# First adaLN chunk and first value weights of the first stage, loaded and multiplied in halves

## The chip, the cores and the metric

The kernel runs on one core of a Trainium2 chip. The core has a matrix engine (PE, or TensorE), a vector engine (DVE), a scalar engine (ACT), a general engine (POOL), and SP, which only issues transfers here. Each engine takes its instructions in a fixed order, and they meet through semaphores. The metric is the device time of one execution in microseconds (us), as the median of several runs.

## The reference

A two-layer backbone over 512 latent tokens and 256 context tokens of width 1024. Each layer first makes, from two conditioning vectors (one for latent, one for context rows), a shift and a scale for every feature, and applies them to the normalised rows:

```python
def adaln_terms(cond, w_ada, b_ada):
    m = jax.nn.silu(cond) @ w_ada + b_ada
    return jnp.split(m, 3, axis=-1)          # shift, scale, gate
...
    xl = rms_norm(h_lat, norm_w[li]) * (1.0 + scale_l[:, None, :]) + shift_l[:, None, :]
    xc = rms_norm(h_ctx, norm_w[li]) * (1.0 + scale_c) + shift_c
...
    au_l, av_l, az_l, bq_l, bk_l, bv_l, bz_l = jnp.split(xl @ w_in, EVEN_SPLITS, axis=-1)
```

The first stage of the kernel computes `xl`, `xc` of layer 0 and, interleaved with it, `av = x @ w_in[:, 512:1024]`, the first of the products with `w_in`. All the rest (gating, differential attention, the second layer, the last norm) comes after that stage and isn't touched.

## The kernel before

Matrices are split into a high part (rounded to the matrix engine's 32-bit format, by ACT) and the low rest (a subtraction, by DVE), so each product takes three matmuls: high·high, high·low, low·high. Names ending in h and l are these two parts: `xh`, `xl` for the features, `wh`, `wl` for weights. Rows are in tiles of 128: six row tiles of tokens (0 to 3 latent, 4 and 5 context), eight tiles of features (`kt`), taken in four pairs j (two tiles i = 0, 1 each).

For each pair j the first stage needs the adaLN chunk j (2 MB of `ada`, in four transfers of 512 KB; before, each of the four holds two tiles of the contraction for all 512 outputs of the chunk: the shift and the scale of both feature tiles) and the value weights of that pair (`wr` from `in_ew`, 512 KB, `wch[j]`). The steps for a pair are: `ada_products` multiplies the chunk with the two conditioning vectors (32 small matmuls, L175, each writing a strip of 32 partitions), DVE copies the rows out (L183), PE turns them (L188), DVE adds and multiplies biases (L198 to L201) into `AD` (shift) and `gT` (scale). Then `turned` turns x (L402), and `modulate_in` makes `xh` on ACT (L414), an unrounded copy `xm` (DVE L418 for latent rows, ACT L420 for context rows) and `xl` on DVE (L423). Last come the value products: `av_first` for the latent rows of pair 0 (L462, 24 matmuls of 128x512), `av_part` otherwise (L79 to L81, through `mm3`).

The order in this place comes from two sources. The block `in_order(ACT, DVE, PE)` fixes the order of these three engines for pair 0 as the code is written; it includes the square sums of the context rows (`ssq_quarter` on ACT, L264; `ssq_vector` on DVE, L381), their root (`rstd_of`, the power on POOL, L156) and their scaling (`normalise`, ACT L395). Behind the block a scheduler of the language orders each engine's instructions by its own estimates. `turn_over(n)` (L446) are n matmuls of the identity whose result nobody reads. `load_w` loads the weights of pair j + 1 into `wr` (two buffers) and `split_w` makes `wh` (ACT L66) and `wl` (DVE L67). SP issues all transfers in program order on one queue: four loads of x, small constants, chunk 0, the value weights of pair 0 (`w0`), the context columns of x, chunk 1, and so on.

Of the kernel before, what the change touches and what calls it, by code (L numbers as in the profile page):

```python
# [11 lines left out]
F32 = mybir.dt.float32  # L12
F32R = mybir.dt.float32r
AF = mybir.ActivationFunctionType
ALU = mybir.AluOpType
# [3 lines left out]
P = 128  # L19
# [11 lines left out]
def tile_backbone(ctx: ExitStack, tc: tile.TileContext, a: dict, out: bass.AP):  # L31
    nc = tc.nc
    PE, ACT, DVE, POOL, SP = nc.tensor, nc.scalar, nc.vector, nc.gpsimd, nc.sync

    cst = ctx.enter_context(tc.tile_pool(name="cst", bufs=1))
    wp = ctx.enter_context(tc.tile_pool(name="wp", bufs=3))
# [72 lines left out]
    ident = cst.tile([P, P], F32, name="ident")  # L109
# [5 lines left out]
    p_bg = pool("bg", "left")  # L115
    p_fill = pool("fill", "right")
    fill(p_fill, "fill2", 136)
    p_in = pool("in", "right")
# [5 lines left out]
    def load_raw(src):  # L124
        raw = wp.tile([P, 1024], F32, tag="raw", name=nm("wr"), bufs=2)
        SP.dma_start(raw, src)
        return raw

    def load_ada(n, pl, bufs):

        res = []
        for c in range(4):
            w = til(pl, [P, 2, 512], F32, "ada", bufs)
            SP.dma_start(w, a["ada"][n, c].rearrange("p (k n) -> p k n", k=2))
            res.append(w)
        return res
# [3 lines left out]
    adab = const("adab", [P, 2, 6, 4])  # L140
    normw = const("normw", [P, 2, 8])
    wch = a["ew"]
    adaw = [load_ada(0, p_in, 12)]
    w0 = load_raw(wch[0])
    for j in range(4):
        load_x(j, 4, 2)
    adaw.append(load_ada(1, p_in, 12))
# [11 lines left out]
    c32 = til(p_bg, [P, 8, 32], F32, "c32")  # L159
# [26 lines left out]
    def ada_rows(li, j, row):  # L186
        ps = tr_ps()
        PE.transpose(ps[:, :P], row, ident)  # L188
        ada_bias(li, j, ps[:, :P].rearrange("p (b v) -> p b v", b=4)[:, :, :2])
# [14 lines left out]

    def ada_chunk(li, j, ws, between=None):
        ada_rows(li, j, ada_products(ws, between))


    ada_rest = [(0, 4), (0, 5), (1, 0)]
# [243 lines left out]
                s = (slice(None), i, slice(t * P, (t + 1) * P))  # L453
                mm3(avb[t], (xh[s], xl[s]), (wh[:, i, :], wl[:, i, :]), j == 0 and i == 0, j == 3 and i == 1)

    def av_first(w, ts):

        (xh, xl), (wh, wl) = XT[0], w
        for n, (x_, w_) in enumerate(((xh, wh), (xh, wl), (xl, wh))):
            for i in range(2):  # L460
                for t in ts:
                    PE.matmul(avb[t], x_[:, i, t * P:(t + 1) * P], w_[:, i, :], start=n + i == 0, stop=False)  # L462


    w0h, w0l = (wp.tile([P, 1024], F32R, tag="w" + s, name=nm("w" + s)) for s in "hl")
# [1 line left out]
    with in_order(ACT, DVE, PE):  # L467
        normalise(0, 0)
        xt0 = []

        def fill_in(kt):
            if kt < 5:
                turn_over(2)
            else:
                i = len(xt0)
                xt0.append(turned(0, 0, i, tr_ps() if i else avb[4]))
        ada_chunk(0, 0, adaw[0], between=fill_in)
        ACT.activation(w0h, w0, AF.Copy)
        turn_over(6)
        modulate_in(0, 0, 0, *XT[0], ps=xt0[0],  # L480
                    between=lambda: DVE.tensor_tensor(w0l, w0, w0h.bitcast(F32), op=ALU.subtract))
        for q in range(1, 4):
            ssq_vector(q, 5)
        second = modulate_in(0, 0, 1, *XT[0], ps=xt0[1], only="h")
        for q in range(4):
            ssq_quarter(xq[q], acc, q, 4, 1 if q else 2)
        rs.append(rstd_of(acc, 4, 2))
        second()
        normalise(1, 0)
        h = normalise(0, 1)  # L490
    ws_in = [(w0h, w0l)]
    w = [x.rearrange("p (k n) -> p k n", k=2) for x in ws_in[0]]
    av_first(w, range(4))
    for i in range(2):
        modulate_in(0, 1, i, *XT[0])
    for j in range(4):
# [44 lines left out]
    for t in range(6):  # L541
        v = gav[t]
# [612 lines left out]
def _layout(i):  # L1155
# [8 lines left out]
    for li in range(2):  # L1164
        W = A["ada_w"][li].T
        for j in range(6):
# [4 lines left out]
            ada.append(W[rows].reshape(4, P, D))  # L1171
            adab.append(A["ada_b"][li][rows])
    r["ada"] = np.stack([w.reshape(512, 4, 2, P).transpose(1, 3, 2, 0).reshape(4, P, 1024) for w in ada])
    r["adr"] = np.concatenate(ada[7:12])
    r["crow"] = np.broadcast_to(c[:, None], (2, P, D))
    r["adab"] = np.stack(adab).reshape(2, 6, 4, P).transpose(3, 0, 1, 2)
# [43 lines left out]
```

## Time and profile before

| | us |
|---|---|
| median of 3 runs (691.6 to 692.15) | 692.09 |
| the profiled execution | 691.32 |
| its span, from the first to the last instruction | 689.4 |
| PE busy in the span | 679.4 (99%) |
| DVE busy | 477.2 (69%) |
| ACT busy | 363.5 (53%) |

The profiled execution has 1.9 us outside its span. The span is one long row of matmuls: PE is busy in 99% of it, and its granted clock is 0.997 of full speed. A busy PE counts a matmul from its start to its modelled end, and matmuls overlap, so the 99% is not a measure of spare time; the waits of PE and the gaps between starts are. The first stage takes about the first 64 us, the rest of the span is not affected by the change in what it computes.

### The profile page before, as it was taken

To read this page: it belongs to the slowest core of one execution; us is meant where nothing else is said; L and a number is where in the kernel's file an instruction comes from. 1 tells how busy PE (TensorE), PEld (TensorE's weight loads), DVE (VectorE), ACT (ScalarE), POOL (GpSimd) and SP (SyncE) were. 2 spreads that over 40 slices of the span, in tenths; PEclk is the share of its full clock that TensorE was granted. 3 is DMA by queue.
4 is the path that set the end of the run, shared out by engine and by line. 5 is a ranking of instruction groups with operands and counts; after the bars stand their busy time and mean duration, and the time that the engine had idled before them with its cause. 6 is when DMAs were issued, how large, how long until landed. Compare 5 with 4: busy or idle time off the path is not lost.

```text
span 689.4 us, 12288 instructions
## 1 busy us (share of the span) xinstructions
PE 679.4 (99%) x5053; PEld 628.9 (91%) x5053; DVE 477.2 (69%) x883; ACT 363.5 (53%) x705; POOL 20.3 (3%) x27
## 2 busy tenths in 40 slices
PE   9999999999999999999999999999999999999996
PEld 8778999989988899898899999988889999999995
DVE  2647839954797947979665328676458898876864
ACT  4956323133567645675534314354458787886422
POOL 1000000010001000010000000010000000000000
PEclk9999999999999999999999999999999999999998
DMA  9965894301101011010623301251210211111402
GB/s 339 408 239 222 307 329 132 114 27 36 62 31 32 0 63 61 32 32 1 244 66 127 99 2 32 63 181 35 88 62 26 68 62 63 31 62 31 123 32 91
DMA packets 20359, 69.90 MB, mean 101 GB/s; under 512 B 3152, under 2 KB 3280, under 8 KB 20304
## 3 DMA queue, kind: packets, MB, share of 16 engines
q1 hardware_dynamic: 20304, 69.13, 28.7%
q8 instruction: 39, 0.64, 0.4%
q14 instruction: 16, 0.13, 0.1%
HBM read 67.02 MB, written 2.10 MB: 100 GB/s over the span
## 4 chain that ended last, share of the span: by engine, by line
PE 91%; DVE 4%; ACT 3%; issue 0%; POOL 0%; POOLq 0%; ACTq 0%; DVEq 0%
PE mm L79 19%; PE mm L81 19%; PE mm L80 19%; PE S L79 5%; PE S L80 5%; PE S L81 5%; PE tr L1024 3%; PE S L663 2%; PE S L665 2%; PE tr L175 2%; PE tr L681 2%; PE S L446 2%; PE S L1002 1%; PE S L1006 1%; PE tr L698 1%; PE tr L293 1%
## 5 line engine op out<-in xcount | busy, mean ns | idle before, releaser
L80 PE MATMUL mm<-xl,wh 128*128 128x512 f32 (+1 forms) x240 | 84.7, 353 | 0.0
L81 PE MATMUL mm<-xh,wl 128*128 128x512 f32 (+1 forms) x240 | 84.5, 352 | 0.0
L79 PE MATMUL mm<-xh,wh 128*128 128x512 f32 (+1 forms) x240 | 84.1, 351 | 0.0
L67 DVE TENSOR_TENSOR wl<-wr,wh 128x1024 fp32r<-128x1024 f32 (+1 forms) x40 | 48.3, 1210 | 38.3 <-ACT wh L66 36.8
L369 ACT ACTIVATE e<-S,s 128x768 f32<-128x768 f32 (+1 forms) x80 | 65.2, 817 | 17.4 <-DVE s L368 17.0
L368 DVE TENSOR_REDUCE s<-S 128x1 f32<-128x768 f32 (+1 forms) x80 | 67.2, 842 | 3.6 <-PE S L1006 1.7
L66 ACT ACTIVATE wh<-wr 128x1024 fp32r<-128x1024 f32 (+1 forms) x40 | 41.8, 1049 | 48.2 <-PE mm L80 21.5
L66 ACT ACTIVATE ah<-tr 128x512 fp32r<-128x512 f32 x76 | 43.9, 595 | 24.9 <-PE tr L681 12.7
L67 DVE TENSOR_TENSOR al<-tr,ah 128x512 fp32r<-128x512 f32 x76 | 50.4, 685 | 7.6 <-ACT ah L66 6.7
L79 PEld LDWEIGHTS mm<-xh,wh 128*128 128x128 f32 x240 | 45.2, 188 | 5.2 <-ACT wh L66 0.2
L79 PE MATMUL mm<-wh,xh 128*128 128x256 f32 (+1 forms) x172 | 49.8, 289 | 0.0
L80 PEld LDWEIGHTS mm<-xl,wh 128*128 128x128 f32 x240 | 45.2, 188 | 4.9
L80 PE MATMUL mm<-wl,xh 128*128 128x256 f32 (+1 forms) x172 | 49.6, 288 | 0.0
L81 PEld LDWEIGHTS mm<-xh,wl 128*128 128x128 f32 x240 | 45.1, 188 | 4.6 <-DVE wl L67 0.2
L81 PE MATMUL mm<-wh,xl 128*128 128x256 f32 (+1 forms) x172 | 49.3, 287 | 0.0
L79 PE MATMUL mm<-wo,xh 128*128 128x256 f32 x144 | 40.6, 282 | 0.0
L81 PE MATMUL mm<-wo,xl 128*128 128x256 f32 x144 | 40.4, 281 | 0.0
L80 PE MATMUL mm<-wo,xh 128*128 128x256 f32 x144 | 40.4, 280 | 0.0
L79 PEld LDWEIGHTS mm<-wh,xh 128*128 128x128 f32 x172 | 32.5, 189 | 0.8 <-issue 0.4
L156 POOL TENSOR_TENSOR s<-s,mhalf 128x6 f32<-128x6 f32 (+4 forms) x15 | 16.0, 1070 | 584.6 <-DVE s L1126 225.2
L81 PEld LDWEIGHTS mm<-wh,xl 128*128 128x128 f32 x172 | 32.4, 189 | 0.5
L80 PEld LDWEIGHTS mm<-wl,xh 128*128 128x128 f32 x172 | 32.4, 188 | 0.5
(337 smaller groups left out, 2008.2 us busy)
## 6 DMA issues: line engine op xcount, KB each, us to landing
ada<-in_ada SPq DMA_DIRECT2D x28, 512.0 KB, 9.1
wr<-in_ew SPq DMA_DIRECT2D x28, 512.0 KB, 3.5
ada<-in_adr SPq DMA_DIRECT2D x12, 512.0 KB, 5.7
wr<-in_ewo SPq DMA_DIRECT2D x8, 512.0 KB, 3.4
wr<-in_owz SPq DMA_DIRECT2D x8, 512.0 KB, 3.6
wr<-in_adr SPq DMA_DIRECT2D x8, 512.0 KB, 3.4
wr<-in_owo SPq DMA_DIRECT2D x8, 512.0 KB, 3.7
xr<-in_x SPq DMA_DIRECT2D x4, 768.0 KB, 7.1
```

The costliest lines, as they stand in the source:

```text
L66: ACT.activation(h, src, AF.Copy)
L67: (eng or DVE).tensor_tensor(l, src, h.bitcast(F32), op=ALU.subtract)
L79: PE.matmul(ps, lh, rh, start=first, stop=False)
L80: PE.matmul(ps, lh, rl, start=False, stop=False)
L81: PE.matmul(ps, ll, rh, start=False, stop=last)
L156: return POOL.tensor_tensor(dst, src, mhalf[:, :n], op=ALU.pow)
L175: PE.matmul(ps[32 * b:32 * b + 32, :P], c32[:, kt, :], ws[kt // 2][:, kt % 2, b * P:(b + 1) * P], start=kt == 0, stop=kt == 7)
L368: mx = DVE.tensor_reduce(nmx[:, :1], v[:, :, :w], axis=AX.XY, op=ALU.max, negate=True)
L369: ACT.activation(e.rearrange("p (c k) -> p c k", k=w), v[:, :, :w], AF.Exp, bias=nmx[:, :1], scale=1.0, accum_out=sm[:, col:col + 1])
L446: PE.matmul(avb[3][:, :P], ident, ident, start=True, stop=True)
L663: PE.matmul(S[:, c, :n], QS[:, m, qs], KS[:, m, k0:k0 + n], start=True, stop=False)
L1024: PE.transpose(ps[:, i * 256 + q * P:i * 256 + (q + 1) * P], es[q][:, (2 * j + i) * P:(2 * j + i + 1) * P], ident)
```

## The change

Chunk 0 is stored in another layout in DRAM: the first two transfers (0 and 1) now hold all eight tiles of the contraction for feature tile i = 0 alone (its shift and its scale), the other two (2 and 3) the same for i = 1. The value weights `w0` are loaded in two transfers of 256 KB, the first half (feature tile 0) between the two halves of the chunk, the second behind them. `half_products(i)` and `half_rows(i)` do for one feature tile what `ada_products` and `ada_rows` did for two, and `av_first(i, ts)` is a generator that yields after each set of four matmuls, so that the products of feature tile 1's shift and scale stand between the value matmuls of feature tile 0. The square sums of the context rows on DVE and ACT move behind the modulation of feature tile 1.

```diff
-    adaw = [load_ada(0, p_in, 12)]
-    w0 = load_raw(wch[0])
+    adaw = [load_ada(0, p_in, 12, (0, 1))]
+    w0 = wp.tile([P, 1024], F32, tag="raw", name=nm("wr"), bufs=2)
+    SP.dma_start(w0[:, :512], wch[0][:, :512])
+    adaw[0] += load_ada(0, p_in, 12, (2, 3))
+    SP.dma_start(w0[:, 512:], wch[0][:, 512:])
...
+    def half_products(i, between=None):
+        ps = tr_ps()
+        for kt in range(8):
+            w = adaw[0][2 * i + kt // 4].rearrange("p k n -> p (k n)").rearrange("p (k n) -> p k n", k=4)
+            for b in range(2):
+                PE.matmul(ps[32 * b:32 * b + 32, :P], c32[:, kt, :], w[:, kt % 4, b * P:(b + 1) * P],
+                          start=kt == 0, stop=kt == 7)
+            if between and kt % 2:
+                between(kt)
+        row = til(p_bg, [P, P], F32, "arow", 2)
+        DVE.tensor_copy(row[:64, :], ps[:64, :P])
+        return row
+
+    def half_rows(i, row):
+        ps = tr_ps()
+        PE.transpose(ps[:, :64], row[:64, :], ident[:64, :64])
+        r = ps[:, :64].rearrange("p (b v) -> p b v", b=2)[:, :, :2]
...
+        DVE.scalar_tensor_tensor(g, r[:, 1, :], adab1[:, 0, 0, i:i + 1], wide(normw[:, 0, i:i + 1]), op0=ALU.add, op1=ALU.mult)
+        DVE.tensor_scalar(AD[:, 0, 0, i, :], r[:, 0, :], adab[:, 0, 0, i:i + 1], None, op0=ALU.add)
...
-    def av_first(w, ts):
-        (xh, xl), (wh, wl) = XT[0], w
-        for n, (x_, w_) in enumerate(((xh, wh), (xh, wl), (xl, wh))):
-            for i in range(2):
-                for t in ts:
-                    PE.matmul(avb[t], x_[:, i, t * P:(t + 1) * P], w_[:, i, :], start=n + i == 0, stop=False)
+    def av_first(i, ts):
+        xh, xl = XT[0]
+        for n, (x_, w_) in enumerate(((xh, w0h), (xh, w0l), (xl, w0h))):
+            for t in ts:
+                PE.matmul(avb[t], x_[:, i, t * P:(t + 1) * P], w_[:, i * 512:(i + 1) * 512], start=n + i == 0, stop=False)
+            yield
...
-        ada_chunk(0, 0, adaw[0], between=fill_in)
-        ACT.activation(w0h, w0, AF.Copy)
+        half_rows(0, half_products(0, between=fill_in))
+        ACT.activation(w0h[:, :512], w0[:, :512], AF.Copy)
         turn_over(6)
-        modulate_in(0, 0, 0, *XT[0], ps=xt0[0],
-                    between=lambda: DVE.tensor_tensor(w0l, w0, w0h.bitcast(F32), op=ALU.subtract))
+        modulate_in(0, 0, 0, *XT[0], ps=xt0[0], between=lambda: DVE.tensor_tensor(
+            w0l[:, :512], w0[:, :512], w0h[:, :512].bitcast(F32), op=ALU.subtract))
+        first = av_first(0, range(4))
+        next(first)
+        row = half_products(1)
+        next(first)
+        half_rows(1, row)
+        next(first)
+        ACT.activation(w0h[:, 512:], w0[:, 512:], AF.Copy)
+        modulate_in(0, 0, 1, *XT[0], ps=xt0[1], between=lambda: DVE.tensor_tensor(
+            w0l[:, 512:], w0[:, 512:], w0h[:, 512:].bitcast(F32), op=ALU.subtract))
+        for _ in av_first(1, range(4)):
+            pass
         for q in range(1, 4):
             ssq_vector(q, 5)
-        second = modulate_in(0, 0, 1, *XT[0], ps=xt0[1], only="h")
         for q in range(4):
             ssq_quarter(xq[q], acc, q, 4, 1 if q else 2)
         rs.append(rstd_of(acc, 4, 2))
-        second()
         normalise(1, 0)
         h = normalise(0, 1)
...
-    av_first(w, range(4))
...
+    r["ada"][0] = ada[0].reshape(2, 2, P, 2, 4, P).transpose(1, 3, 5, 4, 0, 2).reshape(4, P, 1024)
```

In the new file the lines that stay stand lower: `turned` is L431 (before L402), `turn_over` L475 (L446), `xh` L443 (L414), `xm` L447 and L449 (L418, L420), `xl` L452 (L423), the squares on DVE L410 (L381), x scaled on ACT L424 (L395), chunk products L179 (L175); `mm3` keeps L79 to L81. New are L218 (`half_products`), L223 (copy of the rows), L228 (their turning), L234 and L235 (scale and shift), L490 (`av_first`), L507 and L517 (the two halves of `wh` of pair 0), L509 and L518 (of `wl`).

PE, from the end of the first chunk's products to the first value matmuls, before (`ada_115` is the last transfer of chunk 0, `S_186`, `mm_184` and `mm_185` are accumulators of the value products, `x_97` is x of pair 0):

```order
L175 MATMUL tr_234<-ada_115,c_14_139 32x128 x8
L402 MATMUL tr_275<-ident,x_97 128x128 x4
L188 MATMUL tr_282<-ident,arow_280 128x128
L446 MATMUL S_186<-ident 128x128 x6
L462 MATMUL mm_184<-wh_196,xh_38_188 128x512
L462 MATMUL mm_185<-wh_196,xh_38_188 128x512
L462 MATMUL S_186<-wh_196,xh_38_188 128x512 x2
L462 MATMUL mm_184<-wh_196,xh_38_188 128x512
L462 MATMUL mm_185<-wh_196,xh_38_188 128x512
```

The same place on PE now (`ada_109` and `ada_111` hold feature tile 0, `ada_115` and `ada_117` feature tile 1):

```order
L218 MATMUL tr_235<-ada_111,c_14_140 32x128 x4
L431 MATMUL tr_260<-ident,x_97 128x128 x4
L228 MATMUL tr_267<-ident,arow_265 128x64
L475 MATMUL S_187<-ident 128x128 x6
L490 MATMUL mm_185<-wh_197,xh_38_189 128x512
L490 MATMUL mm_186<-wh_197,xh_38_189 128x512
L490 MATMUL S_187<-wh_197,xh_38_189 128x512 x2
L218 MATMUL tr_287<-ada_115,c_14_140 32x128 x8
L218 MATMUL tr_287<-ada_117,c_14_140 32x128 x8
L490 MATMUL mm_185<-wl_198,xh_38_189 128x512
L490 MATMUL mm_186<-wl_198,xh_38_189 128x512
L490 MATMUL S_187<-wl_198,xh_38_189 128x512 x2
```

Half of the chunk's products, and one of two turnings of 64 columns, have moved behind the first four value matmuls.

DVE, from `xm` of feature tile 0 to the context rows' square sums, before (`jk` are the squares, the two rows with `s_317` sum and scale them for the root on POOL):

```order
L418 TENSOR_SCALAR xm_294<-S_187,gT,AD 128x512
L481 TENSOR_TENSOR wl_197<-wr_117,wh_196 128x1024
L423 TENSOR_TENSOR xl_39_189<-xm_294,xh_38_188 128x512
L381 SCALAR_TENSOR_TENSOR jk_299,s_145<-x_98 128x256
L381 SCALAR_TENSOR_TENSOR jk_301,s_145<-x_99 128x256
L381 SCALAR_TENSOR_TENSOR jk_303,s_145<-x_100 128x256
L268 TENSOR_REDUCE s_317<-s_145 128x2
L270 TENSOR_SCALAR s_317<-s_317 128x2
L418 TENSOR_SCALAR xm_305<-tr_275,gT,AD 128x512
L423 TENSOR_TENSOR xl_39_189<-xm_305,xh_38_188 128x512
```

The same place on DVE now:

```order
L452 TENSOR_TENSOR xl_39_190<-xm_278,xh_38_189 128x512
L223 COPY arow_304<-tr_287 64x128
L234 SCALAR_TENSOR_TENSOR gT<-tr_310,adab_145,normw_sb 128x2
L235 TENSOR_SCALAR AD<-tr_310,adab_sb 128x2
L447 TENSOR_SCALAR xm_319<-tr_260,gT,AD 128x512
L518 TENSOR_TENSOR wl_198<-wr_113,wh_197 128x512
L452 TENSOR_TENSOR xl_39_190<-xm_319,xh_38_189 128x512
L410 SCALAR_TENSOR_TENSOR jk_336,s_146<-x_98 128x256
L410 SCALAR_TENSOR_TENSOR jk_338,s_146<-x_99 128x256
L410 SCALAR_TENSOR_TENSOR jk_340,s_146<-x_100 128x256
L297 TENSOR_REDUCE s_352<-s_146 128x2
L299 TENSOR_SCALAR s_352<-s_352 128x2
```

The square sums of the context rows stand behind `xm`, `wl` and `xl` of feature tile 1, where they stood ahead of its `xm` and `xl`.

ACT, behind the block that fixes the order, before (`wr_370` are the value weights of pair 1, `wr_498` those of pair 2; `xh_40` is `xh` of pair 1; `x_99` and `x_100` are x of pairs 2 and 3):

```order
L66 ACTIVATE wh_372<-wr_370 128x1024
L395 ACTIVATE x_99<-x_99,s_180 128x256 x4
L395 ACTIVATE x_99<-x_99,s_319 128x256 x2
L414 ACTIVATE xh_40_190<-tr_424,AD,gT 128x512
L414 ACTIVATE xh_40_190<-tr_433,AD,gT 128x512
L395 ACTIVATE x_100<-x_100,s_180 128x256 x2
L414 ACTIVATE xh_40_190<-tr_442,AD,gT 128x256
L395 ACTIVATE x_100<-x_100,s_180 128x256
L414 ACTIVATE xh_40_190<-tr_449,AD,gT 128x256
L420 ACTIVATE xm_445<-tr_442,AD,gT 128x256
L420 ACTIVATE xm_452<-tr_449,AD,gT 128x256
L66 ACTIVATE wh_500<-wr_498 128x1024
```

The same place on ACT now (`wr_379` is pair 1, `wr_507` pair 2):

```order
L66 ACTIVATE wh_381<-wr_379 128x1024
L424 ACTIVATE x_99<-x_99,s_181 128x256 x4
L424 ACTIVATE x_99<-x_99,s_354 128x256 x2
L66 ACTIVATE wh_509<-wr_507 128x1024
L443 ACTIVATE xh_40_191<-tr_433,AD,gT 128x512
L443 ACTIVATE xh_40_191<-tr_442,AD,gT 128x512
L424 ACTIVATE x_100<-x_100,s_181 128x256 x3
L443 ACTIVATE xh_40_191<-tr_451,AD,gT 128x256
```

The scheduler has put the high part of pair 2's weights ahead of `xh` of pair 1; on DVE the low part (`wl_510`, L67) stands in the same way ahead of `xm` of pair 1. From the last value matmuls of the stage on, the engines' orders are the same as before.

## Rows read from the trace of the kernel before

**Rows 1.** The page, block 1: busy us, share of the span, instructions.
```profile
PE 679.4 (99%) x5053; PEld 628.9 (91%) x5053; DVE 477.2 (69%) x883; ACT 363.5 (53%) x705; POOL 20.3 (3%) x27
```

**Rows 2.** Waits of PE, whole span: line, releaser, us in total, times, longest.
```profile
PE tr L402 <- ACT x L395: 0.4, 1, 0.4
PE tr L188 <- DVE arow L183: 0.2, 1, 0.2
```

**Rows 3.** Windows: stretch, length, busy by engine, granted clock, DMA share, GB/s.
```profile
17.50:25.00 7.50, 7.11 (x33) 4.96 (x37) 5.57 (x14) 6.84 (x21) 0.70 (x1) 1.00 1.03 410
...
683.00:685.00 2.00, 0.00 (x0) 0.00 (x0) 1.14 (x4) 0.51 (x2) 0.48 (x1) 1.00 0.00 0
...
686.00:687.50 1.50, 0.00 (x0) 0.00 (x0) 0.00 (x0) 0.00 (x0) 0.00 (x0) 0.50 0.62 257
```

**Rows 4.** Chain that ended last, in time: start, us, engine, tile, line.
```profile
11.21 0.57 PE tr L175 x16
11.79 0.64 PE S L446 x4
...
14.22 0.59 PE S L402 x4
...
20.05 1.05 DVE jk L381 x6
...
30.16 0.23 PE S L81
```

**Rows 5.** Timeline, 15 to 18 us: start, us, engine, line, operation, idle before and releaser.
```profile
15.20 1.06 ACT L478 ACTIVATE wh<-wr 128x1024 fp32r<-128x1024 f32 x1 [2.25 <-DMA wr<-in_ew]
...
15.80 0.32 PE L188 MATMUL tr<-ident,arow 128*128 128x128 f32 x1
...
15.96 1.50 PE L446 MATMUL S<-ident 128*128 128x128 f32 x12
16.16 0.16 DVE L198 TENSOR_TENSOR AD<-tr,adab_sb 128x4 f32<-128x4 f32 x1 [0.42 <-PE tr L188]
...
16.43 0.16 DVE L201 TENSOR_TENSOR gT<-gT,normw_sb 128x4 f32<-128x4 f32 x1
16.69 0.78 ACT L414 ACTIVATE xh<-S,AD,gT 128x512 fp32r<-128x512 f32 x1 [0.43 <-DVE gT L201]
...
17.52 0.73 PE L462 MATMUL mm<-wh,xh 128*128 128x512 f32 x2
```

**Rows 6.** Timeline, 17.5 to 27 us.
```profile
17.50 0.81 DVE L418 TENSOR_SCALAR xm<-S,gT,AD 128x512 f32<-128x512 f32 x1 [0.91 <-ACT xh L414]
...
18.23 1.22 DVE L481 TENSOR_TENSOR wl<-wr,wh 128x1024 fp32r<-128x1024 f32 x1
...
19.36 0.69 DVE L423 TENSOR_TENSOR xl<-xm,xh 128x512 fp32r<-128x512 f32 x1
19.50 0.30 PEld L462 LDWEIGHTS mm<-wl,xh 128*128 128x128 f32 x2 [0.28 <-DVE wl L481]
...
21.63 0.70 POOL L156 TENSOR_TENSOR s<-s,mhalf 128x2 f32<-128x2 f32 x1 [10.41 <-DVE s L270]
...
22.37 1.31 ACT L395 ACTIVATE x<-x,s 128x256 f32<-128x256 f32 x3 [0.64 <-POOL s L156]
...
23.70 0.56 ACT L414 ACTIVATE xh<-tr,AD,gT 128x256 fp32r<-128x256 f32 x1
...
24.87 1.95 PE L175 MATMUL tr<-ada,c 128*32 128x128 f32 x64
```

**Rows 7.** Timeline, 25 to 35 us: pair 1, and the weights of pairs 1 and 2.
```profile
25.91 1.06 ACT L66 ACTIVATE wh<-wr 128x1024 fp32r<-128x1024 f32 x1
...
29.44 1.45 ACT L414 ACTIVATE xh<-tr,AD,gT 128x512 fp32r<-128x512 f32 x2
...
33.88 1.06 ACT L66 ACTIVATE wh<-wr 128x1024 fp32r<-128x1024 f32 x1
```

**Rows 8.** Transfers issued from 21.8 to 22.0 us: times, KB each, us to landing.
```profile
wr<-in_ew SPq DMA_DIRECT2D x1, 512.0 KB, 10.2
```

More of the change, by code (lines that the diff above doesn't have):

```diff
@@ L127, in load_raw, with load_ada @@
         return raw
-    def load_ada(n, pl, bufs):
+    def load_ada(n, pl, bufs, parts=range(4)):
         res = []
-        for c in range(4):
+        for c in parts:
             w = til(pl, [P, 2, 512], F32, "ada", bufs)
@@ L206, in ada_chunk, with wide @@
         ada_rows(li, j, ada_products(ws, between))
+    def half_products(i, between=None):
[14 more added lines that the diff above has]
+        r = ps[:, :64].rearrange("p (b v) -> p b v", b=2)[:, :, :2]
+        def wide(x):
+            return x.to_broadcast([P, 2])
+        g = gT[:, 0, i, :]
+        DVE.scalar_tensor_tensor(g, r[:, 1, :], adab1[:, 0, 0, i:i + 1], wide(normw[:, 0, i:i + 1]), op0=ALU.add, op1=ALU.mult)
+        DVE.tensor_scalar(AD[:, 0, 0, i, :], r[:, 0, :], adab[:, 0, 0, i:i + 1], None, op0=ALU.add)
     ada_rest = [(0, 4), (0, 5), (1, 0)]
@@ L491, in tile_backbone @@
     ws_in = [(w0h, w0l)]
-    w = [x.rearrange("p (k n) -> p k n", k=2) for x in ws_in[0]]
-    av_first(w, range(4))
     for i in range(2):
```

## The prediction

> **What bounds the kernel now.** I read the page's busy times first: PE 679.4 of 689.4 us, every other engine far below [rows 1]. So what a change gives or costs is what it does to the row of PE's matmuls: work added to it, work taken from it, and gaps. Then PE's waits: over the whole span only single short ones are named, and two of them, 0.4 and 0.2 us, lie in the first stage [rows 2]. Then the stage itself, in the chain and the timeline [rows 4 to 7]. Transfers run at 410 GB/s there with all engines of the queue busy, and the clock is granted in full [rows 3]. Behind the stage PE waits for almost nothing, and the order there is unchanged, so a shift of PE at the end of the first stage, about 64 us, is a shift of the end of the kernel. The sum is made there.
>
> **Start of the value products (a gain of 0.95 us).** Before, PE goes at 11.21 through four groups of chunk products (0.57 each), two of two identity matmuls (0.64) and two of four turnings (0.59): 11.21 + 2.28 + 1.28 + 1.18 = 15.95 [rows 4]. Now each group has half its matmuls. A group of 16 records isn't half as long when halved: the 64 records of the next chunk take 1.95 us with a tail of some 0.27, so 0.026 each [rows 6], 0.42 for 16, and the rest of the 0.57 is the switch. Half a group is then 0.21 + 0.15, say 0.37 (bounds 0.285 and 0.57). Four of them save 0.8 (0 to 1.14): the turning of the rows stands at 15.15. Three small DVE steps from 16.16 to 16.59, the last waiting for the one ahead [rows 5], become two that don't wait for each other: 0.18 less. So `xh`, 16.69 before, starts at 15.71, takes 0.78, and the first value matmul comes at 16.55 instead of 17.52 [rows 5]. The six identity matmuls ahead, 1.50 long with the tail, move with the turning and end at 16.5: they only just don't bind. The transfers allow it: all of `w0` landed at 15.2 [rows 5], and at 410 GB/s its first half lands two chunk transfers (1.28 each) and half a weight transfer (0.64) earlier, near 12.0, three us ahead of its use.
>
> **Work that moves behind that start (+1.2).** Sixteen chunk products (32 records, 0.83) now stand after the first four value matmuls, with a switch into and out of them (0.18 each). The bounds are 0.83 and two whole groups plus a switch, 1.3. The chunk's last transfer lands half a weight transfer ahead of 15.2, at 14.6, long before 17.7, when it is needed.
>
> **The chain of feature tile 1 (+0.6).** From 16.55: four matmuls at 0.23 [rows 4] to 17.5, products to 18.5, four with `wl` from 18.7 to 19.65, then the turning of the second rows. Its scale is ready on DVE 0.6 later (0.36 from the turning to the first step, as from 15.80 to 16.16 [rows 5], and 0.25 for two), at 20.25; `xh` of tile 1 takes 0.78, to 21.05. PE has four matmuls in the meantime, to 20.65: it waits 0.4. Four with high weights end at 22.0. Those with the low weights need `xm` (0.73 to the next start, 17.50 to 18.23 [rows 6]) and half of a subtraction of 1.22, at most as long as the 0.69 of `xl` [rows 6]: 21.1 + 0.73 + 0.69 = 22.5, a wait of 0.5. Before, one wait of 0.28 stood in this stretch [rows 6]. 0.4 + 0.5 - 0.3 = 0.6 (0 to 1.2).
>
> **The context rows (+1.8).** This is the largest term, and the change makes it by the place of the square sums. `xl` of tile 1 ends on DVE at 23.1. Only then come three squares (1.05 for them, [rows 4]), the sum and its scaling (0.45, 21.1 to POOL's start at 21.63 with their gaps), the power on POOL (0.70) [rows 6], and the first context tile on ACT (0.5): 23.1 + 1.05 + 0.45 + 0.7 + 0.05 + 0.5 = 25.9. PE has finished all 24 value matmuls by 24.4, and the next in its row is the turning of those tiles: a wait of 1.5, against 0.4 now [rows 2]. Before, four value matmuls (0.93) stood behind these turnings and covered the 0.56 of the context `xh` [rows 6]. Now that cover is gone, since the value matmuls have all been done, and PE waits for it, 0.7 with the hand-over. 1.5 + 0.7 - 0.4 = 1.8 (0.9 if ACT and DVE overlap better than I add them, 2.2 if worse).
>
> **Pair 1 (a gain of 0.2).** The wait of 0.2 for the copied rows [rows 2] goes, since PE comes later to it (0 to 0.2).
>
> **Pair 2's weights ahead of pair 1 (+1.4).** In the new order ACT makes the high part of pair 2's weights before `xh` of pair 1. Before, from POOL's end at 22.33 to the start of pair 1's weights on ACT is 3.6 us, and from there to `xh` of pair 1 3.5 [rows 6, 7]. From 25.35 now, ACT would be free for `xh` at 32.4. Pair 2's weights, issued at 21.89, land 10.2 later, at 32.1 [rows 8]; so ACT hardly waits for them, but spends 0.95 of the 1.06 [rows 7] on them, and `xh` ends at 34.05. PE reaches the matmul that needs it at 33.25 by the same count (27.3, when it goes on after the context rows, and 12 matmuls, the 64 records and nine turnings, with a wait of 0.14): a wait of 0.8. On DVE the low part (1.22) stands ahead of `xm` of pair 1, which frees the two banks for the next turnings: two more waits, 0.45 and 0.15. Together 1.4 (0 if PE is later than I count; one for one more if the transfer lands later). Nothing else is new on SP: pair 2's load waits for DVE's second half, until 22.5 instead of 21.89, and eight transfers are queued ahead of it.
>
> **Sum.** -0.95 + 1.2 + 0.6 + 1.8 - 0.2 + 1.4 = +3.85. On the profiled execution's 691.32 that is 695.2; it ran 0.77 under the median, so on the median of 692.09 it is **695.9**.
>
> One page speaks against the split of the load. In this trace transfers queue: a load issued at 21.89 needs 10.2 us to land because others are ahead of it [rows 8], and the stretch moves 410 GB/s [rows 3], so one more transfer of the same bytes costs nothing here. The Trainium skill, "DMA: Bandwidth & Descriptors", section "Anatomy of one DMA", gives each transfer of the software path a fixed cost of about 2.0 us. By that, if it held for this queue and didn't overlap, pair 2's weights would land 2 us later; the trace does not bear it out, but a late landing is a rival below, priced from rows.
>
> **Rivals.** (a) Pair 2's conversion is covered, because PE gets to pair 1 later than I count: the sum loses 1.4, +2.45, 694.5. For it: my count of PE there is the longest in the working; against it: the same count would have to be 0.8 too short. (b) Pair 2's weights land later. The landing at 32.1 is right at ACT's need at 32.35, so every further us is a us for PE; with the length of a 512 KB transfer and a half (1.9), +1.6 more: 697.5. Against it: the bytes and their order ahead of it are the same. (c) **Faster**: the early start stands and the vector chain closes behind it. It decides at the context turnings: if the power on POOL is done by the time PE has its 24 matmuls behind it, 24.4 less 0.5, so by 23.9 instead of 25.35, and tile 1's chain by 0.5 earlier, PE keeps 0.95, pays 0.35 for the switches alone (the products themselves only moved), and loses the waits of before (0.3 + 0.4 + 0.2): 692.09 - 0.95 + 0.35 - 0.9 = 690.6. Against it: the chain is a sum of measured durations on one engine after the other, and 1.45 us of 3 would have to vanish. (d) Halfway between, near no change. (e) The clock falls in the new gaps. At the end of the span PE does nothing from 683 on; the clock is still granted in full to 685, and is 0.50, its level of 1.2 GHz, from 686 to 687.5 [rows 3]. My longest gap is 1.5 us, between full rows of work. If it fell, a matmul of 0.23 would take twice that; over some thirteen of them +3, so 698.9. The Trainium skill, "TensorE: Matmul & The Clock Gate", section "Why this matters for your kernels", asks for no longer idle gaps between bursts of matmuls; by that rule these gaps are too short, and the sum stays.
>
> **How the numbers follow.** Forecast 0.62, (a) 0.15, (b) 0.09, (c) 0.07, (d) 0.04, (e) 0.03. The forecast's own range, with its bounds, is 694.6 to 697.2. The range has to take in (a) with its lower bounds and (b): 693.2 to 697.8, which leaves out (c), (d), (e) and the tails. A measurement of this kernel tells 0.2%, 1.4 us, from no change. Slower by more than that: forecast, (a), (b), (e) less their low ends, 0.86; the same 0.07; faster 0.07.
>
> **What the changed profile would show.** First value matmul (L490) at 16.5 to 16.7. Its second set of four behind the products at 18.7. PE's waits: for ACT x (L424) about 1.5 at the context turnings near 26, 0.7 behind it, 0.4 and 0.5 in tile 1. ACT's conversion of pair 2's weights (L66) at 32.3, with `xh` of pair 1 right behind it near 33.3, and L79 of pair 1 near 34.0 after a wait of 0.8. The first 128x256 matmul 3.5 to 4 us later than before, and from there on the same distances as before. The sum would be wrong if that lag shrank later, that is if something behind the stage had been waiting for a fixed time, or if the waits for the context rows are not there.

## The result, and the profile after

The changed kernel takes 698.88 us (median of four runs, 698.21 to 699.62) beside 692.12 of the kernel before: 1.0104 times as long, interval 1.0092 to 1.0116. That is slower, as forecast, but by 6.8 us and not by 3.85, and outside the range of 693.2 to 697.8. The profiled execution took 698.21, its span 696.0 (691.32 and 689.4 before).

The timeline of the changed kernel (start us, us, engine, line, operation, in brackets the idle time ahead and what ended it); its rows answer [rows 4 to 7]:

```profile
10.31 0.63 PE L218 MATMUL tr<-ada,c 128*32 128x128 f32 x8
10.87 0.71 PE L475 MATMUL S<-ident 128*128 128x128 f32 x4
...
15.83 0.78 ACT L443 ACTIVATE xh<-S,AD,gT 128x512 fp32r<-128x512 f32 x1 [2.27 <-DVE AD L235]
...
16.66 0.73 PE L490 MATMUL mm<-wh,xh 128*128 128x512 f32 x2
...
17.78 1.94 PE L218 MATMUL tr<-ada,c 128*32 128x128 f32 x32
...
22.36 0.73 PE L490 MATMUL mm<-wh,xh 128*128 128x512 f32 x2 [0.17 <-ACT xh L443]
...
23.80 0.73 PE L490 MATMUL mm<-wl,xh 128*128 128x512 f32 x2 [0.25 <-DVE wl L518]
...
25.93 0.70 POOL L160 TENSOR_TENSOR s<-s,mhalf 128x2 f32<-128x2 f32 x1 [14.63 <-DVE s L299]
...
27.23 0.84 PE L431 MATMUL tr<-ident,x 128*128 128x128 f32 x4 [1.30 <-ACT x L424]
...
28.62 0.79 PE L79 MATMUL S<-wh,xh 128*128 128x512 f32 x1 [0.55 <-ACT xh L443]
...
29.77 2.94 PE L179 MATMUL tr<-ada,c 128*32 128x128 f32 x64
...
33.56 1.05 ACT L66 ACTIVATE wh<-wr 128x1024 fp32r<-128x1024 f32 x1
...
35.20 1.45 ACT L443 ACTIVATE xh<-tr,AD,gT 128x512 fp32r<-128x512 f32 x2 [0.59 <-DVE gT L205]
...
38.66 0.50 PE L79 MATMUL S<-wh,xh 128*128 128x512 f32 x1 [0.44 <-ACT xh L443]
...
69.92 0.28 PE L79 MATMUL mm<-wh,xh 128*128 128x256 f32 x1
```

Four things are to be seen. A group of half the products (8 records, two for each of its four matmuls) stands 0.56 ahead of what follows it, where a whole group of 16 took 0.57 [rows 4]; the second half's 32 records take 1.94, as long as the 64 of a whole chunk [rows 6]. PE waits for the context rows, 1.30 and 0.55. Right behind that, the same 64 records take 2.94 instead of 1.95. And the first 128x256 matmul, with which the rest of the kernel begins, comes at 69.92 instead of 63.95: 5.97 of the 6.6 by which the span grew lie in the first stage.

The windows of the changed kernel (length, busy time of the engines, then the granted clock, DMA share, GB/s) say why the 64 records took longer (the first row is for later):

```profile
4.50:6.00 1.50, 1.50 (x15) 1.50 (x15) 0.78 (x4) 0.91 (x4) 0.00 (x0) 1.00 1.01 407
...
26.00:27.00 1.00, 0.00 (x0) 0.00 (x0) 0.00 (x0) 0.33 (x1) 0.64 (x1) 1.00 1.02 406
27.00:28.00 1.00, 0.77 (x4) 0.40 (x4) 0.00 (x0) 0.98 (x3) 0.00 (x0) 1.00 1.03 401
28.00:29.00 1.00, 0.45 (x2) 0.38 (x2) 0.00 (x0) 1.00 (x3) 0.00 (x0) 0.71 1.03 414
29.00:31.00 2.00, 2.00 (x26) 1.27 (x29) 0.85 (x2) 2.00 (x5) 0.00 (x0) 0.50 1.02 408
31.00:32.00 1.00, 1.00 (x32) 0.94 (x28) 0.70 (x1) 1.00 (x4) 0.00 (x0) 0.58 1.04 414
32.00:40.00 8.00, 7.56 (x63) 5.89 (x52) 5.04 (x11) 7.20 (x16) 0.00 (x0) 1.00 1.02 406
```

PE's busy time (first number behind the length) is 0.00, 0.77 and 0.45 in the three us from 26 on; in the third of them the clock falls (0.71 on average), and behind them it is 0.50, its level of 1.2 GHz. Summed over the windows the clock is missing 0.29 + 2 x 0.50 + 0.42 = 1.7 us.

### The profile page after: what moved, and what is told of

Same layout as the page of the kernel before. It is cut to its first block, busy times and chain, and to the rows that moved or that the text cites. A ratio compares the mean times of both kernels' runs of the same rounds, so it can differ in the third digit from the quotient of the medians.

```text
span 696.0 us, 12298 instructions
## 1 busy us (share of the span) xinstructions
PE 683.5 (98%) x5054; PEld 631.2 (91%) x5054; DVE 477.5 (69%) x886; ACT 363.9 (52%) x706; POOL 20.3 (3%) x27
## 4 chain that ended last, share of the span: by engine, by line
PE 92%; DVE 4%; ACT 3%; issue 0%; POOL 0%; POOLq 0%; ACTq 0%; DVEq 0%
PE mm L79 19%; PE mm L81 19%; PE mm L80 19%; PE S L79 5%; PE S L81 5%; PE S L80 5%; PE tr L1060 3%; PE S L699 2%; PE S L701 2%; PE tr L179 2%; PE S L475 2%; PE tr L717 1%; PE S L1038 1%; PE S L1042 1%; PE tr L734 1%; PE tr L322 1%
## 5 line engine op out<-in xcount | busy, mean ns | idle before, releaser
L81 PE MATMUL mm<-xh,wl 128*128 128x512 f32 (+1 forms) x240 | 84.4, 352 | 0.0
L79 PE MATMUL mm<-xh,wh 128*128 128x512 f32 (+1 forms) x240 | 84.3, 351 | 0.0
L67 DVE TENSOR_TENSOR wl<-wr,wh 128x1024 fp32r<-128x1024 f32 (+1 forms) x40 | 48.2, 1208 | 37.6 <-ACT wh L66 36.0
L67 DVE TENSOR_TENSOR al<-tr,ah 128x512 fp32r<-128x512 f32 x76 | 50.3, 684 | 7.7 <-ACT ah L66 6.7
L79 PE MATMUL mm<-wh,xh 128*128 128x256 f32 (+1 forms) x172 | 49.8, 290 | 0.0
L79 PEld LDWEIGHTS mm<-xh,wh 128*128 128x128 f32 x240 | 45.2, 188 | 5.1 <-ACT wh L66 0.2
L81 PEld LDWEIGHTS mm<-xh,wl 128*128 128x128 f32 x240 | 45.2, 188 | 4.8
L81 PE MATMUL mm<-wh,xl 128*128 128x256 f32 (+1 forms) x172 | 49.3, 288 | 0.0
L79 PE MATMUL mm<-wo,xh 128*128 128x256 f32 x144 | 40.6, 282 | 0.0
L81 PE MATMUL mm<-wo,xl 128*128 128x256 f32 x144 | 40.4, 281 | 0.0
L79 PEld LDWEIGHTS mm<-wh,xh 128*128 128x128 f32 x172 | 32.5, 189 | 0.9 <-ACT vnh L66 0.2
L81 PEld LDWEIGHTS mm<-wh,xl 128*128 128x128 f32 x172 | 32.4, 189 | 0.5
```

Of the source, the lines that this page charges most:

```text
L67: (eng or DVE).tensor_tensor(l, src, h.bitcast(F32), op=ALU.subtract)
L79: PE.matmul(ps, lh, rh, start=first, stop=False)
L81: PE.matmul(ps, ll, rh, start=False, stop=last)
```

## The experiments

Differences are each to the kernel before on the same chip (691.2 to 692.1).

| | us | to before | ratio, interval |
|---|---|---|---|
| changed kernel | 698.88 | +6.8 | 1.0104 [1.0092, 1.0116] |
| e1 squares early | 694.41 | +2.6 | 1.0041 [1.0027, 1.0054] |
| e2 gap filled, ten | 698.48 | +6.7 | 1.0106 [1.0092, 1.0119] |
| e3 four strips | 694.93 | +3.1 | 1.0051 [1.0038, 1.0063] |
| e4 before, groups in two passes | 691.63 | -0.2 | 1.0000 [0.9991, 1.0009] |
| e5 before, late squares | 693.86 | +2.7 | 1.0038 [1.0025, 1.0050] |
| e6 chunk whole, weights in halves | 692.72 | +1.5 | 1.0019 [1.0011, 1.0028] |
| e7 e1 and e3 together | 693.94 | +2.7 | 1.0044 [1.0032, 1.0056] |
| e8 early start | 692.03 | +0.8 | 1.0014 [1.0005, 1.0023] |
| e9 pair 2's weights held | 697.60 | +5.6 | 1.0082 [1.0069, 1.0095] |
| e10 gap filled, five | 696.24 | +4.2 | 1.0062 [1.0049, 1.0074] |
| e11 early start 2 | 690.29 | -1.8 | 0.9975 [0.9966, 0.9983] |
| e12 before, long rows in two passes | 700.41 | +8.4 | 1.0119 [1.0105, 1.0134] |

### What half the products cost

The theory: the four strips of 32 partitions that a chunk's products write work side by side, and time goes by the matmuls of one strip. The rival, on which the prediction had counted: each record costs its 0.026.

**e3, four strips.**

```diff
+                r0 = 32 * (b + 2 * (kt % 2))
-                PE.matmul(ps[32 * b:32 * b + 32, :P], ..., start=kt == 0, stop=kt == 7)
+                PE.matmul(ps[r0:r0 + 32, :P], ..., start=kt < 2, stop=kt > 5)
...
-        PE.transpose(ps[:, :64], row[:64, :], ident[:64, :64])
+        PE.matmul(ps[:, :64], row, ident2, start=True, stop=True)
```

> The changed kernel with its half products spread over four strips of 32 partitions instead of two: even contraction tiles write strips 0 and 1, odd ones strips 2 and 3, and the turning of the rows becomes a matmul with two stacked identities of 64, which also adds the two sums. The number of product matmuls is the same, with half as many one behind the other in each strip. Theory A (strips run side by side, a group costs by its contraction steps in one strip): the first half's four groups of 0.57 become some 0.33 each, and the second half's 16 products take 1.0 instead of 1.94; -0.9 and -0.9 as far as PE is the bound there, 698.9 - 1.8 = 697.1, less if the vector chain takes it over. Rival B (a product costs by itself, wherever it is written): the groups stay at 0.57 and 1.94, 698.9.

Its timeline:

```profile
11.80 0.42 PE L221 MATMUL tr<-ada,c 128*32 128x128 f32 x8
12.15 0.71 PE L478 MATMUL S<-ident 128*128 128x128 f32 x4
...
18.51 1.08 PE L221 MATMUL tr<-ada,c 128*32 128x128 f32 x32
...
27.08 0.84 PE L434 MATMUL tr<-ident,x 128*128 128x128 f32 x4 [1.30 <-ACT x L427]
...
28.46 0.50 PE L79 MATMUL S<-wh,xh 128*128 128x512 f32 x1 [0.55 <-ACT xh L446]
...
29.12 1.96 PE L181 MATMUL tr<-ada,c 128*32 128x128 f32 x64
```

The same 8 records now take 0.35 to the next start instead of 0.56, the same 32 take 1.08 instead of 1.94. Theory A. The kernel gained 3.7 and not 1.8; the waits for the context rows are the same 1.30 and 0.55, but the 64 records behind them take 1.96: the clock stayed full in this profile. That, 1.7, and a wait of 0.44 in pair 1 that is gone (under e9) are about the rest.

**e4, the groups of before in two passes.**

```diff
+    def two_passes(ws, between):
...
+        for c in range(4):
+            for h in range(2):
+                for k in range(2):
+                    for b in range(2 * h, 2 * h + 2):
...
-        ada_chunk(0, 0, adaw[0], between=fill_in)
+        ada_rows(0, 0, two_passes(adaw[0], fill_in))
```

> The kernel before, with each of the four groups of chunk 0's products (two contraction tiles by four strips) in another order: strips 0 and 1 for both contraction tiles, then strips 2 and 3 for both. The same matmuls, none added. Theory A (time goes by contraction steps, the strips side by side, so two strips cost as much as four): a group of 0.57 takes about 1.05, four of them +1.9 on the path to the first value matmul: 692.1 + 1.9 = 694.0. Rival B (0.026 for each of a group's records and a fixed switch, as the prediction counted): the groups stay at 0.57, 692.1. Rival C (the groups get longer but transfers or the vector chain behind them hide it): longer groups, and 692.1 to 693.

```profile
11.25 0.66 PE L193 MATMUL tr<-ada,c 128*32 128x128 f32 x16
11.84 0.71 PE L460 MATMUL S<-ident 128*128 128x128 f32 x4
```

0.59 for a group, 691.63: no change, as rival B had it, and a miss for what I had concluded from theory A. It doesn't bring back B's price for a record, which e3 excludes. A group has two matmuls in each strip in either order. So the matmuls for two strips that stand ahead do not, in a group of eight, keep the other two strips idle.

**e12, the long rows of before in two passes.**

```diff
+            todo = [(kt, b) for h in (0, 2) for kt in range(8) for b in (h, h + 1)]
-        for kt in range(8):
-            for b in range(4):
+        for kt, b in todo:
```

> The kernel before, with the products of every chunk that is multiplied in one uninterrupted row of 32 matmuls (64 records) in another order: strips 0 and 1 for all eight contraction tiles, then strips 2 and 3. The same matmuls. Six chunks of the whole kernel. Theory A (strips run side by side only as far as the next matmul in the row can start; sixteen matmuls of two strips ahead block the others): a row takes 3.7 instead of 1.95, and the kernel 691.2 + 6 x 1.8 = 702. Rival B (each strip has its own row and the order is of no account): 1.95 each, 691.2.

The groups by line (busy us, mean ns) of the kernel before and of this one, all chunk products in each, and one of its rows in the timeline:

```profile
L175 PE MATMUL tr<-ada,c 128*32 128x128 f32 x448 | 14.3, 275 | 0.0
```

```profile
L178 PE MATMUL tr<-ada,c 128*32 128x128 f32 x448 | 22.3, 275 | 0.0
```

```profile
24.25 3.29 PE L178 MATMUL tr<-ada,c 128*32 128x128 f32 x64
```

3.29 instead of 1.95 a row, 8.0 more for all (22.3 against 14.3), 8.4 more measured. With sixteen matmuls in two strips ahead, the others do idle, though less than fully (3.9 would be twice). Two half passes one behind the other would take 2 x 0.63 = 1.26 for a group and 2 x 1.94 = 3.88 for a row; measured are 0.66 (e4) and 3.29. Each time has a short tail, which the sums count twice, so some 0.5 to 0.6 is saved in both. A limit on how far ahead in its row PE starts matmuls of idle strips would give that; no run shows the limit itself. The Trainium skill, "TensorEngine Tiling (Array Packing)", section "Key Properties", says that tiles operate independently and that different ones can run matmuls in parallel; the 1.08 against 1.94 agrees, the 3.29 doesn't, and for a row in that order the measurement decides.

**e6, chunk whole, weights in halves.** `load_ada(0, p_in, 12)`, `ada_chunk` and the old layout again; `av_first`, the loads of `w0` and the late squares stay.

> The changed kernel with the chunk whole again (its layout, one row of 32 products, one turning of the rows); the weights stay in halves, the value matmuls in two sets, the squares late. Theory A (the half products are the largest cost: 1.94 for the second half, with nothing saved on the first): PE loses 1.94 of products and one turning, the chain of tile 1 loses its wait for rows, so the context rows come some 2.5 earlier and the clock stays full: 698.9 - 1.9 - 0.4 - 1.7 = 694.9, the remaining difference from before being the late squares. Rival B (the split of the weights is what costs, the products only move): 697 to 698.9.

692.72, 2.2 less than theory A's number. Its first value matmul is at 17.64, its context turnings wait 0.42 and 0.55 behind them, and the clock is full. So the halves of the chunk carry 5.3 of the 6.8, with all that follows from them (the order of pair 2's weights, under e9, too); halving weights and value matmuls costs 1.5 with the late squares included.

### The wait for the context rows, and the clock

**e5, late squares in the kernel before.** `second()` is called ahead of the squares.

> The kernel before with one part of the change alone: the square sums of the context rows stand behind feature tile 1's modulation. Nothing is halved. Theory A (the place of the squares is a cost by itself): three squares of 0.35 on DVE start 1.4 later, the power on POOL too, and the context turnings come about 24.3 instead of 22.9; the last value matmuls fill some 0.4 of it, so a wait of 0.8 to 1.3 and 0.5 for xh behind it: 691.8 + 1.0 to 1.6 = 693.1. Rival B (the squares cost only in company with the late second half; here the value matmuls still queued cover it): 691.8 to 692.2, no wait above 0.5.

Its timeline and windows:

```profile
24.36 0.84 PE L402 MATMUL tr<-ident,x 128*128 128x128 f32 x4 [0.88 <-ACT x L395]
25.75 0.50 PE L79 MATMUL S<-wh,xh 128*128 128x512 f32 x1 [0.55 <-ACT xh L414]
...
26.41 3.37 PE L175 MATMUL tr<-ada,c 128*32 128x128 f32 x64
```

```profile
27.00:30.00 3.00, 3.00 (x54) 2.62 (x46) 1.83 (x3) 3.00 (x8) 0.00 (x0) 0.50 1.01 404
...
252.00:255.00 3.00, 3.00 (x16) 3.00 (x16) 0.19 (x2) 0.60 (x1) 1.32 (x1) 0.51 0.00 0
```

Theory A: waits of 0.88 and 0.55, as counted. The runs also give the clock's price within one kernel. Those with a mean clock of 0.997 and 0.998 took 692.76 and 692.65; three with 0.995 took 693.7 to 694.2; the profiled one, 0.992 with the two falls above, took 695.69. So some 1.3 to 1.5 each, if those with 0.995 had one fall, and a fall in some executions of a kernel, not in all.

**e1, squares early in the changed kernel.** `ssq_vector` and `ssq_quarter` move ahead of `av_first(0, ...)`, `rstd_of` behind `half_rows(1, row)`.

> The changed kernel with one part undone: the square sums of the context rows on DVE and ACT go back ahead of feature tile 1's modulation (behind feature tile 0's), their root stands behind the second half's rows; halves of the chunk and of the weights stay. Theory A (the late squares make the gap of 1.3 us ahead of the context turnings and 0.55 behind them, and the clock falls because of these): both gaps shrink to under 0.5 together, the clock stays granted in full to 32 us, so 1.4 for the gaps and 1.7 for the 3.41 us at half clock go: 698.9 - 3.1 = 695.8. Rival B (the clock falls for another reason, the halves themselves): only the gaps go, 697.5, and a stretch of 3.4 us at 0.50 is still there. Rival C (three squares of 0.35 on DVE ahead of the second half's rows only push the waits into tile 1's chain): 698.9, with new waits of PE at the value matmuls near 22 to 24.

```profile
27.35 0.60 PE L431 MATMUL tr<-ident,x 128*128 128x128 f32 x4
28.53 0.50 PE L79 MATMUL S<-wh,xh 128*128 128x512 f32 x1 [0.58 <-ACT xh L443]
...
29.20 1.95 PE L179 MATMUL tr<-ada,c 128*32 128x128 f32 x64
```

The wait of 1.30 is gone, the second of 0.58 stays, the clock is full: 4.2 less, to +2.6. Theory A, and 1.4 below its number; pair 2's weights, which stand elsewhere in this run (under e9), can be a part of that.

**e2 and e10, the gap filled.**

```diff
         for _ in av_first(1, range(4)):
             pass
+        for _ in range(10):                  # e10: range(5)
+            PE.matmul(avb[4][:, :P], ident, ident, start=True, stop=True)
```

> The changed kernel and nothing undone; ten more identity matmuls, whose result nobody reads, stand on PE between the last value matmul and the context turnings, where PE has a gap of 1.3 us. They do no useful work. Theory A (the gap lets the clock fall): the granted clock stays at 1.00 from 26 to 32 us, the context turnings start within 0.2 of where they did, and the 3.41 us at half clock are given back: 698.9 - 1.7 = 697.2. Rival B (the clock falls for what stands ahead of it or behind it, not for this gap): the same stretch at 0.50, 698.9 or a little more.

In e2 the clock was granted in full there, but ten such matmuls took 2.23 us (26.39 to 28.62), longer than the gap of 1.3 that they were to fill. Behind them stands a wait of 1.22, since the scheduler set the conversion of pair 1's weights (28.89, 1.04 us on ACT) ahead of the context `xh` here. What the clock gave was lost to these two: 698.48, inconclusive by its time.

> The changed kernel with five identity matmuls (ten were too many: they took 2.25 us and pushed the context turnings 0.85 past their time) in the gap of 1.3 ahead of the context turnings. They do no useful work. Theory A (the clock's fall costs 1.7 for each 3.41 us, and the filled gap prevents it): no stretch at 0.50 between 20 and 40 us, and 698.9 - 1.7 = 697.2. Rival B (the clock's share is smaller than that; the ten matmuls lost nothing beyond it): 698.5 again.

The timeline of e10:

```profile
11.04 0.63 PE L218 MATMUL tr<-ada,c 128*32 128x128 f32 x8
...
17.39 0.73 PE L490 MATMUL mm<-wh,xh 128*128 128x512 f32 x2
...
26.53 1.28 PE L523 MATMUL S<-ident 128*128 128x128 f32 x10
27.99 0.95 PE L431 MATMUL tr<-ident,x 128*128 128x128 f32 x4 [0.18 <-ACT x L424]
29.64 0.50 PE L79 MATMUL S<-wh,xh 128*128 128x512 f32 x1 [0.70 <-ACT xh L443]
...
30.30 1.96 PE L179 MATMUL tr<-ada,c 128*32 128x128 f32 x64
...
34.35 1.45 ACT L443 ACTIVATE xh<-tr,AD,gT 128x512 fp32r<-128x512 f32 x2
35.69 1.05 ACT L66 ACTIVATE wh<-wr 128x1024 fp32r<-128x1024 f32 x1
```

The context turnings come no earlier behind the first value matmul than in the changed kernel (10.60 against 10.57), all the work is there and more, and the kernel is 2.6 faster. Not all of that is the clock: the wait of 0.44 in pair 1 isn't there, because the scheduler set pair 2's weights (35.69) behind the first two `xh` of pair 1, as e9 below does by hand. That leaves some 2. Against e9 itself, which has that order and whose clock fell, e10 is 1.4 faster, with an interval of some 1.2 to either side. So the fall that the gap had cost is worth 1.4 to 2. Theory A. All six runs had a mean clock of 0.998 or 0.999; the four of the changed kernel 0.994 to 0.996.

### Pair 2's weights

**e9, held back** with `issue_after` behind the first two `xh` of pair 1.

> The changed kernel with pair 2's weight conversion held back behind the first two xh of pair 1, on ACT and with it on DVE; nothing else. Theory A (as the trace of the changed kernel reads: ACT waited for gT, so the conversion was covered on ACT, and only DVE's low part stands ahead of xm of pair 1, with one wait of 0.44): 698.9 - 0.4 = 698.5. Rival B (as the prediction counted): -1.4, 697.5. Rival C (nothing at all): 698.9.

The wait of 0.44 for `xh` in pair 1 is gone; from the first matmul behind chunk 1's products to the first 128x256 matmul the profile has 36.80 us instead of 37.29, so 0.5. The clock fell here too, from 30 to 33. The median is 1.3 lower, its interval some 1.2 wide to either side, so time alone doesn't tell A from B; the rows tell for A. Nor does the clock alone set a run's time: one run with a mean clock of 0.999 took 697.13, one with 0.994 took 697.01.

The scheduler chooses this order anew for each version. In e1, e3, e6, e7 and e10 pair 2's weights stand behind the first two `xh` of pair 1 without having been held, and the wait of 0.44 is gone. So what those runs gained over the changed kernel has e9's 0.5 in it (1.3 by the medians), beside what their edits did.

### Both causes undone, and a version that uses the halves

**e7, e1's and e3's edits together.**

> The changed kernel with both edits that were tried one at a time: half products over four strips, and the squares back ahead of tile 1. Apart they gave 4.5 and 4.0 of 6.8, and in each the clock stayed full, which is 1.7 that can be given back only once. Theory A (the causes add up otherwise): 698.9 - 1.7 - 2.8 - 2.3 = 692.1. Rival B (they meet in one wait, that of the context rows, so the second gives only its PE time of some 0.9): 693.5.

693.94, rival B by the number. First value matmul at 16.27, and the context turnings wait for nothing, but PE waits elsewhere: 0.57 for the second rows, since a square on DVE that waits for its columns stands ahead of their copy, 0.32 and 0.25 in tile 1, and 1.48 for `xh` of the context rows:

```profile
25.33 0.60 PE L434 MATMUL tr<-ident,x 128*128 128x128 f32 x4
25.85 1.06 ACT L66 ACTIVATE wh<-wr 128x1024 fp32r<-128x1024 f32 x1 [0.79 <-DMA wr<-in_ew]
26.81 0.55 ACT L446 ACTIVATE xh<-tr,AD,gT 128x256 fp32r<-128x256 f32 x1
...
27.41 0.50 PE L79 MATMUL S<-wh,xh 128*128 128x512 f32 x1 [1.48 <-ACT xh L446]
```

Most of that last wait is not the vector chain's doing. The scheduler set the conversion of pair 1's weights ahead of the context `xh`, where the changed kernel has it behind (30.21), and ACT stood 0.79 for their transfer. The turnings are done at 25.93 and `xh` starts at 26.81, so some 0.9 of e7's time is this order, an estimate from these rows. Without it e7 would stand between the two theories, and whether the two edits add up stays open.

**e8 and e11, early start.** Four strips; the identity matmuls between the groups taken out, so that the first half's products stand right behind their transfers; the rows ahead of the turnings of x; tile 1's low weights ahead of its `xm`; the last two value matmuls behind the context turnings.

```diff
+        row = half_products(0)
+        turn_over(2)
+        half_rows(0, row)
+        xt0 = [turned(0, 0, 0, avb[4]), turned(0, 0, 1, tr_ps())]
+        turn_over(4)
...
+        DVE.tensor_tensor(w0l[:, 512:], w0[:, 512:], w0h[:, 512:].bitcast(F32), op=ALU.subtract)
+        low = modulate_in(0, 0, 1, *XT[0], ps=xt0[1], only="h")
+        ssq_vector(2, 5)
+        low()
+        ssq_quarter(xq[2], acc, 2, 4, 1)     # e11; in e8 it stands ahead of `low = ...`
```

> A version that uses what the halves leave free: half products over four strips; eight of the identity matmuls that stood between and behind the groups taken away, so that the first half's products follow its two transfers (landed near 11.3); the turning of the rows comes ahead of the turning of x; the second half's products behind the first four value matmuls; low weights of tile 1 made ahead of its rows; squares spread around tile 1; the last two value matmuls behind the context turnings. Theory A (the first stage was bound by the start of the value products, and everything behind follows): first value matmul near 14.5 instead of 17.5, 1.1 paid for the second half: 691.8 - 1.9 = 689.9. Rival B (chunk 1 lands near 22.9 whatever stands ahead of it, and PE waits for it): 691.0 to 691.8. Rival C (in the new gaps ahead of the first value matmul the clock falls): 692 to 694, with a stretch at 0.50 near 14 to 20 us.

e8 starts the value products at 14.64, then waits 0.92 for `xh` of tile 1 and 1.46 for the context rows, because ACT stood at squares of columns that had not landed: 692.03, slower than A's and B's numbers.

> The early start once more, with the waits that it showed taken on: the square sums that wait for late columns stand behind xh of tile 1 on ACT instead of ahead of it, one on DVE moves between the copy and the use of the second rows, the last ones go to ACT, and only three of pair 1's four scalings stand ahead of the context rows. Theory A (the two waits of 0.92 and 1.46 were ACT's order): 0.1 and 0.8 remain, 692.0 - 1.4 = 690.6, faster than the kernel before by some 0.8. Rival B (the context columns' landing at 18.8 holds POOL, and so the turnings): only the first wait goes, 691.2, the same as before.

Its timeline:

```profile
10.35 0.65 PE L221 MATMUL tr<-ada,c 128*32 128x128 f32 x16
11.37 0.65 PE L221 MATMUL tr<-ada,c 128*32 128x128 f32 x16 [0.38 <-DMA ada<-in_ada]
...
14.40 0.71 PE L493 MATMUL mm<-wh,xh 128*128 128x512 f32 x2
...
15.50 1.08 PE L221 MATMUL tr<-ada,c 128*32 128x128 f32 x32
...
22.13 0.95 PE L434 MATMUL tr<-ident,x 128*128 128x128 f32 x4 [0.79 <-ACT x L427]
```

The wait in tile 1 is gone, that for the context rows is 0.79, and the kernel takes 690.29: 1.8 us faster than before and 8.6 faster than the changed kernel. Theory A. The halves can pay, once the start that they allow is taken and the squares are not in its way. How much of the 1.8 the moved squares and turnings would give without the halves was not tried.

## Why the prediction was wrong in size

The direction and the mechanism of the context rows were right; the price of half a group was wrong, the value matmuls' own row was counted too short, and the rival of the clock was given far too little.

**Start (forecast -0.95, measured 0).** The step that failed is the price of half a group: 0.37, worked out from 0.026 for a record. It is 0.56, since two strips take as long as four, so halving a group saves nothing. The first value matmul does stand at 16.66, near the 16.55 forecast, but for another reason. The first product already came 0.83 earlier, behind the same 32 identity matmuls. The window from 4.5 to 6 us of the kernel before:

```profile
4.50:6.00 1.50, 1.50 (x9) 1.50 (x8) 0.78 (x4) 0.91 (x4) 0.00 (x0) 1.00 1.04 421
```

PE passed 9 records of identity matmuls there before, and 15 in the first row of the changed kernel's windows above: by that pace it came to full speed earlier in that execution, ahead of all that the change touches (the clock column says 1.00 in both). Over the thirteen profiles the first product stands anywhere from 10.31 to 11.86; in e12, whose code up to there is that of before, at 10.54. e10, whose start was like that of before, has its first product at 11.04 and its first value matmul at 17.39, 6.35 apart; before it was 11.14 and 17.52, 6.38. The two small DVE steps in place of three gave 0.07 and not 0.18: `xh` starts 0.82 behind the turning of the rows (15.01 to 15.83), 0.89 before [rows 5].

**Moved products (forecast +1.2, measured +2.1).** The same price: 1.94 for 32 records, and 0.2 for the second turning.

**Feature tile 1 (forecast waits of 0.4 and 0.5, measured 0.17 and 0.25).** PE came later, so it waited less. The 0.28 that the sum took off as a wait of before is idle time of the weight loads (PEld) [rows 6]; PE's starts around it stand 0.48 and 0.57 apart, where 0.47 is usual, so it held PE by some 0.1. What the sum hadn't at all: each set of four value matmuls that stands by itself takes about 1.12 (16.66 to 17.78) rather than the 0.93 counted, since a fresh row's first two take 0.57 to the next start. Without the waits the 24 value matmuls take 6.8 in all, 6.0 before: 0.8.

**Context rows (forecast 1.5 + 0.7 - 0.4, measured 1.30 + 0.55 - 0.37).** Right in place, cause and nearly in size; e1 takes the first wait away, e5 makes both in the kernel before.

**Pair 1 (forecast -0.2).** The wait for its rows [rows 2] is gone, as forecast.

**Pair 2's weights (forecast +1.4, measured 0.44).** Rival (a) in the main: ACT converts them at 33.56, then waits 0.59 for `gT`. PE was later than I had counted, because of the terms above.

**Clock (given 0.03, measured 1.7 by the granted clock).** This is rival (e). Its 698.9 is the median to the tenth by luck: it gave the fall 3 and not 1.7, and its other terms weren't right. I argued that 1.5 us of gap was short between full rows. The rows show the two waits together, with four turnings between them, and the clock at 0.50 right after. The Trainium skill, "TensorE: Matmul & The Clock Gate", section "Why this matters for your kernels", on which I leaned with a sentence, would call each of them too short; the measurement decides against that. What decides in a given execution stays open: e9 and e3 had the same 1.30 and 0.55; e9's clock fell, e3's didn't.

By these, -0.86 + 2.1 + 0.3 + 0.8 + 1.5 - 0.2 + 0.44 + 1.7 = 5.8, of the 5.97 at the first 128x256 matmul; the -0.86 belongs to that execution. The 0.6 by which the lag grows from there to the end is not attributed; 0.5 of it lies in the last 6 us, behind the last power on POOL (684.52 before, 690.62 after).

## What to carry to other kernels

Price a piece of a packed group by what it leaves idle, not by its share of the records: half the strips of a group cost as much as all. When work is pulled forward, look for what it pushes back on the engines that feed the next wait; here squares of a third of a us each opened a gap on PE. And a gap on PE has two prices, its length and the clock behind it, the second paid only in some executions, so give it a chance of its own in a range. Where a scheduler places instructions, compare the engines' orders before a gain is put down to an edit: here weights' conversions moved along with several of them.

## What was new about the hardware

- Matmuls into different strips of 32 output partitions ran side by side: 32 records in two strips 1.94 us, in four 1.08, 64 in four 1.95. Their order didn't count within a group of eight matmuls (0.59 against 0.57), and did in a row of thirty-two (3.29 against 1.95); in both, some 0.5 to 0.6 us of the second two strips' work ran beside the first two's.
- Two waits of PE of 1.30 and 0.55, with four turnings between them, were followed by a clock of 0.50 in two kernels (the changed one and e9) and by none in a third (e3); filling the first with matmuls that do nothing made the changed kernel 2.6 us faster, of which an order that changed with it has 0.4 to 1.3.
- Behind the same 32 identity matmuls the first product started at 10.31 in one execution, at 11.14 in another and at up to 11.86 in further kernels.
